# Conditioning products taken two k-tiles at a time in a two-layer hybrid backbone

## The chip, the cores and the metric

The kernel runs on one core of one Trainium2 chip. The metric is device time in microseconds from one launch; a run's time is compared with other runs of the same program on the same chip. Five engines matter here: TensorE (PE for the matmuls, PEld for the weight loads that overlap them), VectorE (DVE), ScalarE (ACT), GpSimd (POOL) and SyncE (SP), which in this kernel issues every DMA.

## The reference

Two layers work on 256 latent tokens and 256 context tokens of width 2048, in float32. Each layer starts with the conditioning: `mod = silu(c) @ ada_w + ada_b`, once for the latent and once for the context vector, which gives a shift, a scale and a gate of 2048 values each. Then

```
h = rms_norm(x, pre_norm) * (1 + scale) + shift
p = h @ w_in            # 5888 columns: attention, RWKV-7, pooling and their gates
y = concat(attention, rwkv, pool) @ w_out
x = x + gate * rms_norm(y, post_norm)
```

`ada_w` has 2048 rows and 6144 columns a layer, so the conditioning multiplies two vectors with 100 MB of weights in all: nearly no arithmetic, and a large share of the kernel's 350 MB of DMA traffic. The shift and scale of layer 0 are wanted at once; the gate of layer 0 and all of layer 1 are not wanted before the end of layer 0.

## The kernel before, in words

All the work is written as generators (workers) that yield operations. A `Scheduler` (`run`) keeps a model of each engine's time, takes at each step the ready operation with the best key, and emits it. What comes out is a fixed order of instructions for each engine; at run time every engine goes through its list in that order and waits on semaphores. So a change in one worker can move any instruction of the program.

The main worker (`main_work`) streams `w_in` and `w_out`: each weight tile is split by ACT and DVE into a high and a low float32r half (tiles `sp`), and PE multiplies three times with the activations (`h`) into `acc`. Around these products the scheduler fits the RWKV scan (`scan`, `pr`), attention (`att`) and the rest.

The conditioning is `ada_work`. For layer 0's shift and scale (`ADA_FIRST`, 8 units of one column part each) weight tiles `w2` of 128 x 512 are used, all before 173 us. For the rest (`ADA_REST`, 8 units of two parts each) a k-tile of 128 rows comes as two tiles `wa` of 128 x 512 (256 KB each). The stationary operand is the conditioning pair, 128 rows by 2 columns, so the array is used in the shape 128*32 (the trace shows 128*2): four column strips j = 0 to 3 hold four outputs that run side by side. The first `wa` of a k-tile feeds strips 0 and 1, the second strips 2 and 3, one product of 256 columns each. So a k-tile is four products, a unit 16 k-tiles, and all units together 128 k-tiles, 256 tiles `wa` and 512 products. When the shape of the array changes between two instructions, the scheduler's model lets the array drain first (`array_free`), and holds the conditioning's products back for a while (`HOLD`), so that they don't cut into the main products too soon.

Tiles `wa` are loaded by `loads`, which takes a token for each k-tile; the main worker hands out 7/8 of a token with each weight tile of two column blocks that it has used (`ADA_RATE`). The pool keeps 4 tiles for `wa` and allows up to 8. Loads go through SP's queue in the order of the scheduler, together with `wf` and `pw` (weights of `w_in`), `tp` (the scan's inputs) and the rest.

Of the kernel before, what the change touches and what calls it, by code (L numbers as in the profile page):

```python
# [21 lines left out]
KT = D // 128  # L22
# [3 lines left out]
T = SEQ + CTX  # L26
# [137 lines left out]
def PASSES(l):  # L164
    return (0, 1) if l < DEPTH - 1 else (1,)
# [29 lines left out]
ADA_FIRST = [(0, quad, [r]) for r in range(4) for quad in range(2)]  # L195
ADA_REST = [(l, q, [2 * h, 2 * h + 1]) for l, q in ((0, 2), (1, 0), (1, 1), (1, 2)) for h in range(2)]
ADA_RATE = 7
LEND = ("at",)
AHEAD = (1, 2)
SLOT = 40.0  # L200
# [8 lines left out]
PRIO = {"setup": 6, "start": 6, "scan": 5, "front": 3, "back": 4, "elim": 4, "fin": 4, "evac": 4, "pre": 4, "gate": 4, "att": 4, "rg": 5, "mix": 5, "load": 1, "ada": 3, "wl": 2, "ws": 6, "main": 0, "norm": 6, "turn": 3, "post": 6}  # L209
# [417 lines left out]
class Hybrid:  # L627
    def __init__(self, ctx, tc, a, log=None):
# [25 lines left out]
        self.nsplit, self.nmain, self.covered = 0, 0, 0  # L654
        self.sch.lend = lambda c: LEND if c == "sp" and self.nsplit < self.covered else ()

# [191 lines left out]
    def ada_work(self):  # L848
        V, S, G, T, D_ = self.V, self.S, self.G, self.T, self.D
        yield self.until("cond")  # L850
        for l, quad, part in ADA_FIRST + ADA_REST:
            n = 128 * len(part)
            ps = yield Alloc("ada", (128, 512))
            for k in range(KT):
                yield Until(lambda: len(self.adaq) > 0)
                for i in range(len(part)):
                    if i:
                        yield Until(lambda: len(self.adaq) > 0)
                    w = self.adaq.pop(0)
                    for j in range(4) if n == 128 else (2 * i, 2 * i + 1):  # L860
                        rhs = w[:, j, :] if n == 128 else w[:, :, j % 2, :]
                        yield T.matmul(out=ps[32 * j:32 * j + 2, 0:n], lhsT=self.cs[:, k, :], rhs=rhs, start=(k == 0), stop=(k == KT - 1))
                    self.free(w)
            sb = self.adasb
            for j in range(4):
                if j % 2:
                    yield V.tensor_copy(out=sb[32 * j:32 * j + 2, 0:n], in_=ps[32 * j:32 * j + 2, 0:n])
                else:
                    yield S.copy(out=sb[32 * j:32 * j + 2, 0:n], in_=ps[32 * j:32 * j + 2, 0:n])
            self.free(ps)  # L870
            yield self.until("vecs", l)
            pt = yield Alloc("ada", (128, 512))
            for b in range(len(part)):
                yield T.transpose(out=pt[:, 128 * b:128 * b + 128], in_=sb[:, 128 * b:128 * b + 128], identity=self.k("ident"))
            for b, r in enumerate(part):
                kt = slice(r, KT, 4)
                src = pt[:, 128 * b:128 * b + 128].rearrange("p (j s) -> p j s", j=4)[:, :, 0:2]
                bias = self.vec(l, "ada_b", 16 * quad, 16)[:, kt].unsqueeze(2).to_broadcast([128, 4, 2])
                yield V.tensor_tensor(out=self.ada[l][:, quad, kt, :], in0=src, in1=bias, op=ALU.add)
                if quad == 1:  # L880
                    pn = self.vec(l, "pre_norm", 0, 16)[:, kt].unsqueeze(2).to_broadcast([128, 4, 2])
                    yield V.scalar_tensor_tensor(out=self.mm[l][:, kt, :], in0=self.ada[l][:, 1, kt, :], scalar=1.0, in1=pn,
                                                 op0=ALU.add, op1=ALU.mult)
            self.free(pt)
            if quad == 2 and part[-1] == 3:
                gp = yield Alloc("tl", (128, KT, 2))
                pn = self.vec(l, "post_norm", 0, 16).unsqueeze(2).to_broadcast([128, KT, 2])
                yield V.tensor_tensor(out=gp, in0=self.ada[l][:, 2], in1=pn, op=ALU.mult)
                ps = yield Alloc("ada", (128, 512))
                yield T.transpose(out=ps[0:32, 0:128], in_=gp.rearrange("p k s -> p (k s)"), identity=self.k("ident"))  # L890
                gs = yield Alloc("tl", (32, 128))
                yield S.copy(out=gs, in_=ps[0:32, 0:128])
                yield D_.dma_start(out=self.gpd[l], in_=gs)
                self.free(gp, ps, gs)
                self.flag("gp", l)
            for r in part:
                self.flag("ada", l, quad, r)
# [222 lines left out]
    def main_in(self, l, gi, left):  # L1120
# [4 lines left out]
        for q in range(4):  # L1125
            for name, i, cb, mode, bs in group:
                for hf in range(2):
# [25 lines left out]
                    if l or gi:  # L1153
                        self.tokens(ADA_RATE * len(bs) / 16)
                    if l == 0 and gi:
# [736 lines left out]
    def run(self):  # L1892
        self.adaq, self.wq, self.sq, self.yq = [], [], [], {}
        self.eq, self.aq, self.fq, self.pq = [], [], [], []
        self.hh, self.hl = {}, {}
        self.startq, self.xtq = [[], []], [[], []]
        self.bq, self.zq, self.rgq, self.q2, self.g2 = [], [], [], [], []
        self.rgat, self.mixat, self.ygs, self.mixs = None, None, {}, {}
        self.lora, self.mx, self.kf, self.vf, self.o = {}, {}, {}, {}, {}
        self.h1 = {s: ({}, {}) for s in range(2)}  # L1900
        sch = self.sch
        sch.add("setup", PRIO["setup"], self.setup())
        sch.add("start", PRIO["start"], self.start_work())
        for s in range(2):
            sch.add("turn%d" % s, PRIO["turn"], self.turn_work(s))
            sch.add("mod%d" % s, PRIO["norm"], self.mod_work(s))
        sch.add("scan", PRIO["scan"], self.scan_work())
        sch.add("front", PRIO["front"], self.front_work(), 16)
        sch.add("back", PRIO["back"], self.back_work(), 16)
        sch.add("elim", PRIO["elim"], self.elim_work())  # L1910
        sch.add("fin", PRIO["fin"], self.fin_work(), 16)
        sch.add("evac", PRIO["evac"], self.evac_work())
        sch.add("pre", PRIO["pre"], self.pre_work())
        sch.add("gate", PRIO["gate"], self.gate_work())
        sch.add("att", PRIO["att"], self.att_work(0))
        sch.add("rg", PRIO["rg"], self.rg_work())
        sch.add("mix", PRIO["mix"], self.mix_work())
        for l in range(DEPTH):
            for s in PASSES(l):
                sch.add("post%d%d" % (l, s), PRIO["post"], self.post_work(l, s), 16)  # L1920
        sch.add("load", PRIO["load"], self.loads())
        sch.add("ada", PRIO["ada"], self.ada_work(), 16)
        sch.add("wl", PRIO["wl"], self.w_loads())
        sch.add("ws", PRIO["ws"], self.w_split())
        sch.add("es", 0, self.early_split())
        sch.add("main", PRIO["main"], self.main_work(), 8)
        with self.tc.manual_schedule():
            sch.run()
# [18 lines left out]
```

## Time and profile before

| | us |
|---|---|
| median of 3 runs | 1771.61 |
| lowest, highest | 1769.43, 1776.53 |
| the profiled execution | 1770.03 |
| its span, first to last instruction | 1768.1 |
| PE busy, in the span | 1675.5 (95%) |
| DVE busy | 1350.8 (76%) |
| ACT busy | 926.8 (52%) |

The span is cut into 40 slices on the profile's page; PE shows nine tenths or more in all but the first and the last two. The mean granted clock of TensorE is 0.981 of the full one. The stage in which the `wa` tiles are used begins with their first product at 172.7 us and ends with the last conditioning instruction at 893.8 us. Behind it come the output product of layer 0, layer 1 and the tail.

### The profile page before, as it was taken

How to read it: one execution, taken by the hardware profiler on the slowest of the kernel's cores; microseconds unless marked ns; L12 is line 12 of the kernel's file. 1: busy time of each engine (PE TensorE's matmuls, PEld its weight loads, DVE VectorE, ACT ScalarE, POOL GpSimd, SP SyncE). 2: the span in 40 equal slices, each digit the busy share in tenths (PEclk: the TensorE clock that was granted, in tenths of full speed). 3: DMA queues.
4: the chain of work that ended last, by engine and by line, in shares of the span. 5: the costliest groups of instructions: out<-in, count | busy, mean ns of one | idle time of the engine just before them, and what ended most of it. 6: DMA issues, size and time to landing. Idle time of an engine off the chain costs nothing.

```text
span 1768.1 us, 38232 instructions
## 1 busy us (share of the span) xinstructions
PE 1675.5 (95%) x13658; PEld 1330.3 (75%) x13658; DVE 1350.8 (76%) x4249; ACT 926.8 (52%) x2278; POOL 16.0 (1%) x93
## 2 busy tenths in 40 slices
PE   4999999999999999999999999999999999999977
PEld 3677677666766676667777888899999888888765
DVE  3335888867897869697767685899689999999863
ACT  5324455434554445345446574575455676666541
POOL 0000000000000000000000000000000000000000
PEclk9999999999999999999999999999999999999988
DMA  9993674657364945574669965665434536555642
GB/s 343 362 365 105 206 227 155 225 185 247 120 221 148 277 149 171 170 238 148 207 223 351 328 191 169 199 202 177 147 102 157 155 98 204 153 165 185 215 132 95
DMA packets 218094, 350.03 MB, mean 198 GB/s; under 512 B 22896, under 2 KB 62128, under 8 KB 217904
## 3 DMA queue, kind: packets, MB, share of 16 engines
q1 hardware_dynamic: 217904, 347.60, 60.2%
q8 instruction: 107, 1.75, 0.4%
q14 instruction: 83, 0.68, 0.1%
HBM read 316.54 MB, written 30.97 MB: 197 GB/s over the span
## 4 chain that ended last, share of the span: by engine, by line
PE 72%; DVE 12%; DMA 10%; ACT 2%; issue 2%; SPq 1%; DVEq 0%; POOL 0%; ACTq 0%
PE acc L587 50%; PE scan L587 6%; PE pr L587 5%; PE att L587 5%; PE ada L587 4%; DVE tp L587 3%; DMA wa<-in_ada_w_dram 2%; DVE sp L587 2%; DMA w<-in_ada_w_dram 2%; DVE q L587 1%; DVE rf L587 1%; DMA wf<-in_w_out_dram 1%; DMA wf<-in_w_in_dram 1%; PE st L587 1%; DMA sp<-w 1%
## 5 line engine op out<-in xcount | busy, mean ns | idle before, releaser
L587 PE MATMUL acc<-h,sp 128*128 128x256 f32 (+1 forms) x5088 | 971.1, 339 | 14.1 <-DMA sp<-w 5.6
L587 PEld LDWEIGHTS acc<-h,sp 128*128 128x128 f32 x5088 | 755.4, 190 | 133.9 <-issue 24.3
L587 DVE TENSOR_TENSOR sp<-wf,sp 128x512 fp32r<-128x512 f32 (+1 forms) x568 | 362.4, 664 | 96.4 <-ACT sp L587 90.2
L587 ACT CAST sp<-wf 128x512 fp32r<-128x512 f32 (+1 forms) x624 | 352.3, 603 | 20.8 <-PE acc L587 7.6
L587 PE MATMUL acc<-sp,h 128*128 128x512 f32 x1152 | 284.6, 403 | 2.9 <-DVE sp L587 2.9
L587 PEld LDWEIGHTS acc<-sp,h 128*128 128x128 f32 x1152 | 216.9, 191 | 54.1 <-DVE sp L587 3.8
L587 DVE TENSOR_TENSOR tp<-tp 128x48 f32<-128x48 f32 (+23 forms) x552 | 133.3, 247 | 5.6
L587 DVE TENSOR_TENSOR tp<-dt,tp 128x48 f32<-128x48 f32 (+23 forms) x496 | 112.0, 226 | 5.6
L587 PE MATMUL ada<-wa,cs 128*2 128x256 f32 x1024 | 85.8, 380 | 6.3 <-DMA wa<-in_ada_w_dram 6.2
L587 ACT CAST pw<-pw 128x512 fp32r<-128x512 f32 x56 | 34.8, 621 | 71.8 <-DMA pw<-in_w_in_dram 59.2
L587 ACT COPY sm<-scan 128x128 f32<-128x128 f32 x64 | 17.0, 265 | 104.4 <-PE scan L587 104.0
L587 DVE TENSOR_TENSOR rf<-tp 64x256 f32<-64x256 f32 x176 | 70.2, 421 | 0.4
L587 DVE STREAM_TRANSPOSE dt<-tp 128x1024 f32<-128x1024 f32 x32 | 65.7, 2077 | 0.0
L587 ACT ACTIVATE aq<-att,q 128x512 f32<-128x512 f32 (+1 forms) x48 | 33.9, 707 | 59.8 <-DVE q L587 49.7
L587 ACT COPY rf<-scan 64x128 f32<-64x128 f32 x128 | 33.2, 259 | 55.6 <-PE scan L587 50.8
L587 DVE SCALAR_TENSOR_TENSOR q<-q 128x4 f32<-128x4 f32 (+3 forms) x378 | 58.3, 159 | 4.2
L587 PEld LDWEIGHTS scan<-rf 128*64 128x64 f32 x896 | 37.3, 137 | 26.2 <-issue 9.2
L587 PE MATMUL ada<-w,cs 128*2 128x128 f32 x1024 | 37.0, 296 | 20.5 <-DMA w<-in_ada_w_dram 19.6
L587 DVE COPY adasb<-ada 2x128 f32<-2x128 f32 (+1 forms) x32 | 11.4, 357 | 57.4 <-ACT adasb L587 50.9
L587 DVE TENSOR_TENSOR pw<-pw 128x512 f32<-128x512 f32 x56 | 38.5, 687 | 21.6 <-ACT pw L587 21.3
L587 PE MATMUL scan<-rf 128*64 128x64 f32 x896 | 49.3, 230 | 4.4 <-DVE rf L587 4.1
L587 ACT COPY tp<-rb 32x128 f32<-32x128 f32 x128 | 37.5, 295 | 28.4 <-DVE rb L587 26.9
(154 smaller groups left out, 1965.7 us busy)
## 6 DMA issues: line engine op xcount, KB each, us to landing
wf<-in_w_in_dram SPq DMA_DIRECT2D x384, 256.0 KB, 3.8
wa<-in_ada_w_dram SPq DMA_DIRECT2D x256, 256.0 KB, 4.2
wf<-in_w_out_dram SPq DMA_DIRECT2D x192, 256.0 KB, 4.5
w<-in_ada_w_dram SPq DMA_DIRECT2D x128, 256.0 KB, 5.3
pw<-in_w_in_dram SPq DMA_DIRECT2D x56, 256.0 KB, 4.8
w<-pw SPq DMA_DIRECT2D x56, 256.0 KB, 2.5
sp<-w SPq DMA_DIRECT2D x56, 256.0 KB, 3.2
wf<-in_w_in_dram SPq DMA_DIRECT2D x48, 128.0 KB, 4.4
```

Of the source, the lines that this page charges most:

```text
L587: op.call(**op.args)
```

## The change

`ada_work` collects the tiles of two k-tiles (`ADA_BATCH = 2`, for the units with `wa` alone) before it yields the first product, then yields the products of the second k-tile and after them those of the first, and frees the four tiles together. The group of accumulations starts and stops with the new first and last product. The number of products, tiles and bytes stays the same, and the worker's window stays 16 operations wide.

```diff
+ADA_BATCH = 2
...
             ps = yield Alloc("ada", (128, 512))
-            for k in range(KT):
-                yield Until(lambda: len(self.adaq) > 0)
-                for i in range(len(part)):
-                    if i:
-                        yield Until(lambda: len(self.adaq) > 0)
-                    w = self.adaq.pop(0)
-                    for j in range(4) if n == 128 else (2 * i, 2 * i + 1):
-                        rhs = w[:, j, :] if n == 128 else w[:, :, j % 2, :]
-                        yield T.matmul(out=ps[32 * j:32 * j + 2, 0:n], lhsT=self.cs[:, k, :], rhs=rhs, start=(k == 0), stop=(k == KT - 1))
-                    self.free(w)
+            size = 1 if n == 128 else ADA_BATCH
+            for k0 in range(0, KT, size):
+                ws = []
+                for _ in range(size * len(part)):
+                    yield Until(lambda: len(self.adaq) > 0)
+                    ws.append(self.adaq.pop(0))
+                for z in range(size):
+                    k = k0 + size - 1 - z
+                    for i in range(len(part)):
+                        w = ws[len(part) * (k - k0) + i]
+                        for j in range(4) if n == 128 else (2 * i, 2 * i + 1):
+                            rhs = w[:, j, :] if n == 128 else w[:, :, j % 2, :]
+                            yield T.matmul(out=ps[32 * j:32 * j + 2, 0:n], lhsT=self.cs[:, k, :], rhs=rhs,
+                                           start=(k0 == 0 and z == 0), stop=(k0 + size == KT and z == size - 1))
+                self.free(*ws)
...
-        sch.add("ada", PRIO["ada"], self.ada_work(), 16)
+        sch.add("ada", PRIO["ada"], self.ada_work(), 8 * ADA_BATCH)
```

The orders are the same up to the first `wa` product. Below, `pr` and `scan` are products of the RWKV part, `acc<-h,sp` main products, `ada<-wa,cs` the conditioning. Three places show what moves.

On PE, shortly after the first `wa` products (at 194 us in the trace), the order of before has:

```order
L587 MATMUL acc<-h,sp 128x512 x3
L587 MATMUL pr<-rf 128x128 x8
L587 MATMUL ada<-wa,cs 2x256 x2
L587 MATMUL acc<-h,sp 128x512 x8
L587 MATMUL pr<-rf 128x128 x8
L587 MATMUL ada<-wa,cs 2x256 x2
L587 MATMUL acc<-h,sp 128x512 x4
```

and the changed one at the same place:

```order
L588 MATMUL acc<-h,sp 128x512
L588 MATMUL pr<-rf 128x128 x8
L588 MATMUL acc<-h,sp 128x512 x10
L588 MATMUL pr<-rf 128x128 x8
L588 MATMUL ada<-wa,cs 2x256 x8
L588 MATMUL acc<-h,sp 128x512 x2
L588 MATMUL pr<-c,rf 128x128 x4
```

Two visits to the conditioning, of two products each, became one visit of eight. Over the whole program, the visits to `ada<-wa,cs` are 112 before (11 of 2 products, 76 of 4, 7 of 6, 18 of 8) and 72 now (8 of 2, 8 of 6, 56 of 8), and the changes of the array's shape from one PE instruction to the next, with the shapes that the trace gives each kind of product, are 808 before and 743 now.

On SP, near the start of the stage, the queue of before has pairs:

```order
L587 DMA pw<-in_w_in_dram 128x512
L587 DMA wa<-in_ada_w_dram 128x512 x2
L587 DMA wf<-in_w_in_dram 128x2x128 x3
L587 DMA rkvd_71<-ev 128x512
L587 DMA wa<-in_ada_w_dram 128x512 x2
L587 DMA pw<-in_w_in_dram 128x512
```

and the changed one, a little further along:

```order
L588 DMA pw<-in_w_in_dram 128x512
L588 DMA w_1_74<-pw 128x512
L588 DMA wf<-in_w_in_dram 128x2x128 x2
L588 DMA wa<-in_ada_w_dram 128x512 x4
L588 DMA w_0_75<-pw 128x512
L588 DMA wf<-in_w_in_dram 128x2x128 x3
```

Rows of four `wa` loads in a stretch number 10 before and 21 now; pairs 99 and 75.

The third place is one where the changed order leaves little between load and use, with the tiles' numbers. SP issues four loads in a row:

```order
L588 DMA wf_6330<-in_w_in_dram 128x512
L588 DMA wa_6403<-in_ada_w_dram 128x512
L588 DMA wa_6409<-in_ada_w_dram 128x512
L588 DMA wa_6406<-in_ada_w_dram 128x512
L588 DMA wa_6412<-in_ada_w_dram 128x512
```

and PE takes the batch apart, the third tile's products ahead and the fourth tile's behind two products of the RWKV part:

```order
L588 MATMUL att_6414<-c_136,aq_6400 128x128 x4
L588 MATMUL ada_5430<-wa_6409,cs_133 2x256 x2
L588 MATMUL pr_6152<-tp_6157,bonesr_137 128x256
L588 MATMUL pr_6152<-tp_6428,bonesr_137 128x256
L588 MATMUL ada_5430<-wa_6412,cs_133 2x256 x2
L588 MATMUL ada_5430<-wa_6403,cs_133 2x256 x2
L588 MATMUL ada_5430<-wa_6406,cs_133 2x256 x2
```

Eight of the 64 batches are split so, into a visit of two products and one of six. Within a k-tile the tile that was pushed first still comes first, so the tile that SP issues last here (6412) is not the one that PE takes first (6409).

## Rows read from the trace of the kernel before

**Rows 1.** The page: the span and each engine's busy time.
```profile
span 1768.1 us, 38232 instructions
PE 1675.5 (95%) x13658; PEld 1330.3 (75%) x13658; DVE 1350.8 (76%) x4249; ACT 926.8 (52%) x2278; POOL 16.0 (1%) x93
```

**Rows 2.** Busy time by stretch: length, each engine (instructions), clock, DMA share, GB/s.
```profile
172.70:893.80 721.10, 708.66 (x5580) 500.41 (x5579) 575.92 (x1897) 352.19 (x894) 7.10 (x44) 0.99 0.60 193
...
1055.40:1702.60 647.20, 615.59 (x5634) 556.12 (x5632) 552.41 (x1823) 387.25 (x980) 7.56 (x38) 0.99 0.52 163
```

**Rows 3.** Chain of waits in the stretch 172.7 to 893.8: shares by line.
```profile
by line: PE acc L587 42.1%; PE att L587 7.9%; PE ada L587 7.9%; PE scan L587 7.7%; PE pr L587 6.7%; DMA wa<-in_ada_w_dram 5.2%; DVE tp L587 4.3%; issue 2.4%; DVE sp L587 2.0%; DVE rf L587 1.6%; DMA pw<-in_w_in_dram 1.5%; DVE q L587 1.4%; DM
```

**Rows 4.** Timeline of PE: start, length, instruction; visits of 4, 8, 12, 16 records.
```profile
195.50 0.60 PE L587 MATMUL ada<-wa,cs 128*2 128x256 f32 x4
196.03 2.14 PE L587 MATMUL acc<-h,sp 128*128 128x512 f32 x8
...
283.70 0.61 PE L587 MATMUL ada<-wa,cs 128*2 128x256 f32 x8
284.25 2.13 PE L587 MATMUL acc<-h,sp 128*128 128x512 f32 x8
...
320.20 1.05 PE L587 MATMUL ada<-wa,cs 128*2 128x256 f32 x16
321.18 0.65 PE L587 MATMUL att<-c,aq 128*128 128x128 f32 x4
...
420.60 1.03 PE L587 MATMUL ada<-wa,cs 128*2 128x256 f32 x12
421.56 0.39 PE L587 MATMUL pr<-tp,bonesr 128*128 128x256 f32 x1
```

**Rows 5.** Timeline of PE: one main product ahead of the same shape, and of another.
```profile
270.95 0.39 PE L587 MATMUL acc<-h,sp 128*128 128x512 f32 x1
271.18 0.86 PE L587 MATMUL att<-at 128*128 128x512 f32 x3
271.87 0.40 PE L587 MATMUL acc<-h,sp 128*128 128x512 f32 x1
272.20 0.69 PE L587 MATMUL scan<-rf 128*64 128x64 f32 x16
```

**Rows 6.** Waits by engine in 172.7 to 893.8: us in total, times, longest.
```profile
PE ada L587 <- DMA wa<-in_ada_w_dram: 6.2, 7, 2.2
PE pr L587 <- ACT tp L587: 2.9, 4, 1.3
...
PEld ada L587 <- DMA wa<-in_ada_w_dram: 14.1, 21, 2.7
```

**Rows 7.** Stretch 172.7 to 893.8, the instructions of tile wa alone.
```profile
172.70:893.80 721.10, 85.72 (x1024) 17.04 (x1024) 0.99 0.60 193
```

**Rows 8.** DMA issues: count, KB each, median us from issue to landing.
```profile
wa<-in_ada_w_dram SPq DMA_DIRECT2D x256, 256.0 KB, 4.2
```

**Rows 9.** Timeline of SP and PE near 680 us; idle time and releaser in brackets.
```profile
680.20 0.94 SPq L587 DMA_DIRECT2D wa<-in_ada_w_dram  x2
...
682.39 0.61 PE L587 MATMUL ada<-wa,cs 128*2 128x256 f32 x8 [1.69 <-DMA wa<-in_ada_w_dram]
...
685.23 1.02 PE L587 MATMUL ada<-wa,cs 128*2 128x256 f32 x4 [2.22 <-DMA wa<-in_ada_w_dram]
...
687.22 1.02 PE L587 MATMUL ada<-wa,cs 128*2 128x256 f32 x4
```

**Rows 10.** Busy time by stretch around the same place; the clock stands behind the engines.
```profile
680.00:684.00 4.00, 1.32 (x12) 0.34 (x10) 3.73 (x15) 0.87 (x2) 0.00 (x0) 0.96 0.91 305
684.00:688.00 4.00, 2.77 (x12) 0.90 (x12) 3.94 (x15) 0.67 (x3) 0.48 (x5) 0.50 0.51 158
688.00:692.00 4.00, 4.00 (x21) 3.59 (x20) 3.52 (x11) 2.85 (x7) 0.14 (x4) 0.68 0.46 148
```

## Prediction

> **What bounds the kernel now.** I read the page first, then the busy time by stretch, then the chain of waits in the one stretch that the change touches, and last the timeline of PE there. PE is busy 95% of the span [rows 1]. In the stretch of the `wa` products, 172.7 to 893.8 us, it is busy 708.7 of 721.1 us, and DVE 575.9 us or 80% [rows 2]. So 12.4 us are left in which PE does nothing, and half of it, 6.2 us, is PE itself standing before a `wa` tile that has not landed [rows 6]; the next in that list, a product that waits for ACT, has 2.9 us. The chain of waits says the same with another weight: five groups of PE work make 42.1 + 7.9 + 7.9 + 7.7 + 6.7 = 72.3% of the stretch, the transfer of `wa` 5.2%, and the rest is DVE work, issue and other transfers in small pieces [rows 3]. In such a stretch time goes away in two ways: PE has less to do, or PE stands less before `wa`. The change touches both, and behind it the orders of all engines are shuffled.
>
> **Part 1: fewer visits.** A visit to the conditioning occupies PE from its first product to the start of the next kind of work. The trace records each of these float32 products twice, so 2, 4, 6 and 8 products are 4, 8, 12 and 16 records. The rows give 196.03 - 195.50 = 0.53 us, 284.25 - 283.70 = 0.55, 421.56 - 420.60 = 0.96 and 321.18 - 320.20 = 0.98 us [rows 4]. Two products cost as much as four, and six as much as eight, because the column strips run side by side: the time goes by steps of one k-tile, begun or whole, not by products. With the counts of the two orders:
>
> before: 11 x 0.53 + 76 x 0.55 + 7 x 0.96 + 18 x 0.98 = 5.8 + 41.8 + 6.7 + 17.6 = 71.9 us;
> now: 8 x 0.53 + 8 x 0.96 + 56 x 0.98 = 4.2 + 7.7 + 54.9 = 66.8 us.
>
> That is 5.1 us less. The eight split batches are the reason that it isn't more: each pays 0.53 + 0.96 instead of 0.98.
>
> **Part 2: fewer changes of shape.** What a change of shape costs the work ahead of it shows in one pair: a main product ahead of another of the same shape takes 271.18 - 270.95 = 0.23 us to the next start, and one ahead of a `scan` product 272.20 - 271.87 = 0.33 us [rows 5], so 0.10 us. The changes fall from 808 to 743, and 65 x 0.10 = 6.5 us. Not all of the 65 are in the stretch: the fall there is larger, and some of it is given back in the output product of layer 0, where scan pieces now stand. The bounds of this term are 0 (if the drain only moves idle time) and 8 us (all 80 changes that 40 visits have at their two ends). I take the 6.5, since the row is an exact pair.
>
> **Part 3: the waits for wa.** The 1024 records of `wa` keep PE busy for 85.7 us [rows 7], and a free run of the same visits would take the 71.9 us of part 1. A visit's last record ends about 0.06 us after the next work starts (0.61 against 0.55), so 112 x 0.06 = 7 us of the 85.7 overlap with the next work. That leaves about 7 us lost inside visits, beside the 6.2 us ahead of them, so some 13 us are in this term; the weight loads' own 14.1 us [rows 6] is the same waiting seen from the other queue and isn't added. A load takes 4.2 us to land [rows 8]. Batching has two effects on it. There are 64 batches to wait for instead of 128 k-tiles, and behind the youngest k-tile the older two tiles are there already. On the other side, a batch waits for the youngest of four tiles instead of two, the four are freed together, and so the next four loads are issued together and closer to their use, as the third place of the order shows. The lower bound is 0, all 13 us gone; the upper bound is twice the present, 26 us, if each batch waits as long as two k-tiles did. I take no change, 13 us, because loads, bytes, tokens and the number of kept tiles are the same, and since the present rows are the nearest to either end.
>
> What stands behind a waiting product is the whole of PE: main products, scan and attention alike, since PE goes through its list in order. DVE is at 80% there and would be the next to be late. SP is passed by more rows of four loads, a megabyte each; the scan's inputs (`tp`) and the weights (`wf`) stand behind those. With the DMA engines at a share of 0.60 in the stretch [rows 2] I cost that at nothing; if the cover is gone, it shows as PE or ACT waiting for `wf` or `tp`.
>
> **Sum.** 5.1 + 6.5 + 0 = 11.6 us of PE work. Of a saving on PE the chain passes on its PE share at least, 72.3% [rows 3]: 8.4 us; all of it would be 11.6. Since PE is busy over 98% of this stretch, I take a value between, 10 us. The profiled execution took 1770.0 us, 1.9 more than its span, and lies 1.6 us under the median of the runs. 1770.0 - 10 = 1760.0, and with the 1.6 us to the median 1761.6. Forecast: 1762 us.
>
> **Stage behind 893.8 us.** Nothing of the change is there, but the order is new. The later stretch has PE idle for 647.2 - 615.6 = 31.6 us [rows 2], more than twice that of the earlier one. A shuffle can move some of that either way; I cost it at nothing and keep 8 us on either side, a quarter of that idle time, as an estimate for the range.
>
> **The rivals.**
>
> First, the saving is handed back as waits. What speaks for it: 28% of the chain in the stretch isn't PE [rows 3], and DVE is at 80%; work that PE no longer hides lets DVE or ACT end last. What speaks against it: PE waited there for others for only 6 us beside `wa`. With half of the 11.6 us kept, 1771.6 - 5.8 = 1766 us, no difference that a measurement of this kernel can tell (about 0.5%, 9 us). Chance 0.35.
>
> Second, the split batches stand and cost the clock. This is the case on the other side. The trace shows its price at one place: two loads issued at 680.20, their products and the next ones start at 682.39 and 685.23 after idle times of 1.69 and 2.22 us [rows 9], and then the granted clock is 0.50, the lower of its two levels (1.2 GHz), in 684 to 688, and 0.68 on average in 688 to 692 [rows 10]; a visit that takes 0.60 then takes 1.02 [rows 4, 9]. Idle time of 1.7 + 2.2 and about 3 us of half speed make 7 us for one place. The order has eight split batches, each with loads issued in a row of four at the most, and a few whole ones with little between load and use. Without the loss of the 13 us changing elsewhere, the gain of 11.6 is gone with two more such places, and the kernel is slower by over 0.5% from three on; with four it is 1771.6 - 11.6 + 28 = 1788 us. Against it: the mean clock of the stretch is 0.99 [rows 2], so half speed lasts at most 0.01 x 721 / 0.5 = 14 us in it, two such places among 112 visits, and those of before may go. Chance 0.14.
> The Trainium skill speaks for this rival: "TensorE: Matmul & The Clock Gate", section "HAM oscillation — how this bites in real kernels", holds that short runs of matmuls between waits for DMA let the clock fall back, and that the fall is paid at each such wait. The trace agrees at 684 us (0.50 behind the two waits) and not in the rest of the stretch, whose mean is 0.99. By that rule, at each of the eight splits, the sum would be 8 x 7 = 56 us worse; by the rows it is one place in 721 us, and I keep the rows.
>
> Third, the waits go too. If one wait for a batch catches the rest, most of the 13 us goes with the 11.6: 1771.6 - 11.6 - 11 = 1749 us. For it: waits are fewer, 64 for 128. Against it: the loads are issued closer to their use. Chance 0.10.
>
> That the change doesn't do what it says is half true already: within a k-tile the older tile still goes first, so in a split batch PE doesn't wait for the youngest tile first. It costs what part 1 has for the splits.
>
> **How the numbers follow.** The forecast has a chance of 0.41, the first rival 0.35, the second 0.14, the third 0.10. Of the forecast's 0.41 a small part, 0.03, lies within 0.5% of before. Faster by over 0.5%: 0.38 + 0.10 = 0.48; within 0.5%: 0.35 + 0.03 = 0.38; slower: 0.14. The range goes from 1750, next to the third rival, to 1774: the first rival's 1766 with the 8 us of the later stage. The second rival is left out above it, and part of the third below.
>
> **What would show it.** In the profile of the changed kernel, right: visits of 16 records at 0.98 us, 56 of them, and PE busy on `wa` at about 80 us or less; PE busy in the whole span down by some 10 us; the stretch from the first `wa` product to the last conditioning instruction shorter by about 10 us; idle time before `wa` near 6 us. Wrong: PE idle before `wa` above 15 us or stretches of the clock at 0.50 beside the one of before (second rival); PE's busy time down and its idle time up by as much on DVE or ACT (first rival); a later stage that moves by more than 8 us, which would mean that the shuffle decides and not the visits.

## The result, and the profile after

| | before | after |
|---|---|---|
| median, us | 1771.98 (4 runs) | 1785.95 (4 runs) |
| lowest, highest | 1769.43, 1776.53 | 1783.34, 1788.66 |
| the profiled execution, and its span | 1770.03, 1768.1 | 1786.87, 1784.8 |

The ratio of after to before is 1.0082, with a 95% interval of 1.0060 to 1.0104. The changed kernel is 14 us slower, where 10 us faster was forecast.

The profile answers in the order of the prediction's steps. First the busy time by stretch (columns as in [rows 2]) of the changed kernel: the old stretch of the `wa` products, the same up to the new last conditioning instruction at 884.5, and the later stretch from the start of layer 1 to its last `scan` product, which holds the same PE work as in [rows 2] (5633 records for 5634). The last row has the instructions of `wa` alone, PE and PEld:

```profile
172.70:893.80 721.10, 704.89 (x5594) 511.91 (x5596) 577.14 (x1900) 355.14 (x897) 7.09 (x44) 1.00 0.61 195
172.70:884.50 711.80, 695.59 (x5524) 505.26 (x5524) 573.80 (x1892) 352.23 (x890) 7.09 (x44) 1.00 0.62 196
1054.30:1720.00 665.70, 625.67 (x5633) 565.79 (x5631) 553.19 (x1823) 388.76 (x980) 7.62 (x38) 0.96 0.50 159
...
172.70:893.80 721.10, 75.08 (x1024) 21.25 (x1024) 1.00 0.61 195
```

The conditioning's stretch is 721.1 - 711.8 = 9.3 us shorter, and PE is busy there for 708.7 - 695.6 = 13.1 us less. The two stretches don't hold quite the same work, though: after's has 64 `scan` records fewer, which PE does later (16 of them in a row take 0.6 to 0.8 us, so some 3 us). The records of `wa` take 75.1 us for 85.7 [rows 7]. A visit of 16 records lasts as long as before (next start less start, 0.97 us in the pair below, from PE's timeline of after):

```profile
323.72 1.04 PE L588 MATMUL ada<-wa,cs 128*2 128x256 f32 x16
324.69 0.96 PE L588 MATMUL acc<-h,sp 128*128 128x512 f32 x3
```

The waits that end PE's idle time in 172.7 to 893.8 (us in total, times, longest), against [rows 6]:

```profile
PE att L588 <- DVE aq L588: 4.6, 5, 2.8
PE ada L588 <- DMA wa<-in_ada_w_dram: 3.5, 4, 1.8
PE pr L588 <- ACT tp L588: 3.4, 4, 1.7
```

So the wait before `wa` did not grow, it fell from 6.2 to 3.5 us. PE's busy time in the whole span did not fall, however: 1675.2 us for the 1675.5 of [rows 1]. Up to here the change did what it says. To see where the gain went I compared the start of the k-th main product (`acc`) in both traces (6240 in each). Offsets are start in the kernel less start in before, in us, worked out from the traces, one execution of each kernel:

```
k of the main product    1950   2210   2340   2730   4680   5070   5200   5590   5720    end
its start in before     818.6  912.9  943.9 1042.9 1361.3 1470.5 1495.3 1580.6 1605.6
after                   -12.1  -10.0   -6.5   -1.1   -0.3  -15.2   +9.8   +1.5  +17.4  +16.8
```

Two losses stand in this line. Of the 10 us by which after is ahead at 913 us, 9 are gone by 980 us, where layer 0 ends. The other 18 us are lost in the second half of layer 1, at two places.

**The end of layer 0.** The chain of waits in 880 to 985 us (start, length, what), of before and then of after:

```profile
927.78 18.12 PE acc L587 x77
945.99 5.96 DMA y<-mixd
...
958.03 5.43 DMA y<-gpd
```

```profile
912.73 5.47 DMA pw<-in_w_in_dram
...
919.72 5.70 DMA pw<-in_w_in_dram
...
928.39 5.36 DMA wf<-in_w_out_dram
933.83 6.07 DMA pw<-in_w_in_dram
...
942.68 5.76 DMA y<-mixd
948.46 0.63 ACT h L588
949.13 8.09 PE acc L588 x28
957.22 5.22 DMA y<-gpd
```

The tiles `y` are filled here from two places: `mixd` is the mixed output of layer 0, the input of the output product, and `gpd` is layer 0's gate, which the conditioning made. Both were written to memory and are read back by the same queue that brings the weights. In after PE was ready earlier, but the chain goes through a row of weight loads, the read of `mixd`, 8 us of main products and the read of `gpd`, and this last one starts at 957.22 for 958.03. The busy time by stretch shows what the transfers had left there, before and then after:

```profile
940.00:980.00 40.00, 37.91 (x157) 30.02 (x156) 28.39 (x47) 25.34 (x50) 0.00 (x0) 0.96 1.03 361
```

```profile
940.00:980.00 40.00, 34.30 (x133) 26.61 (x132) 29.43 (x48) 27.04 (x53) 0.00 (x0) 0.91 1.01 346
```

The DMA engines are full in both (shares of 1.03 and 1.01), and part of what PE had gained stands there as idle time: 40.0 - 34.3 = 5.7 us for 2.1. At main product 2470, behind this place, both kernels have done the same work but for one record, before and then after:

```profile
172.70:978.10 805.40, 790.87 (x5992) 564.81 (x5992) 634.82 (x2010) 400.95 (x992) 7.10 (x44) 0.99 0.63 205
```

```profile
172.70:977.00 804.30, 782.39 (x5991) 571.37 (x5992) 637.24 (x2015) 405.54 (x998) 7.09 (x44) 0.99 0.65 208
```

So for equal work PE is busy 8.5 us less, and idle 21.9 us for 14.5: of the saving, 1.1 us is left. That the transfers hold the end of layer 0 is read from these rows; no run tests it alone.

**Layer 1.** The loss begins behind main product 4680, at 1361 us. PE's busy time from there to the last `scan` product, of before and then of after:

```profile
1361.30:1702.60 341.30, 315.87 (x3154) 276.27 (x3153) 303.13 (x1095) 214.53 (x578) 4.18 (x21) 0.98 0.50 159
```

```profile
1361.00:1720.00 359.00, 325.87 (x3154) 285.77 (x3152) 304.24 (x1095) 216.46 (x578) 4.12 (x21) 0.93 0.48 151
```

The same 3154 records of PE take 17.7 us more: the idle time goes from 25.4 to 33.1 us, and the busy time from 315.9 to 325.9, at a clock of 0.93 for 0.98. PE's timeline at the first place (start, length, idle time and releaser in brackets), of after:

```profile
1467.09 1.68 PE L588 MATMUL att<-aq,at 128*128 128x256 f32 x12
1475.97 1.12 PE L588 MATMUL scan<-c,ts 64*64 64x64 f32 x16 [7.20 <-DVE ts L588]
...
1480.30 2.71 PE L588 MATMUL acc<-h,sp 128*128 128x256 f32 x11
```

and the same two pieces of work in before:

```profile
1459.83 1.58 PE L587 MATMUL att<-aq,at 128*128 128x256 f32 x12
1461.24 5.93 PE L587 MATMUL acc<-h,sp 128*128 128x256 f32 x49
...
1467.56 0.68 PE L587 MATMUL scan<-c,ts 64*64 64x64 f32 x16
```

In before 49 main products stand between the attention and the `scan` product that needs DVE's `ts`; in after none do, and PE stands for 7.2 us. The clock follows (stretches of after, the clock third from the end):

```profile
1471.00:1476.00 5.00, 0.03 (x2) 0.06 (x2) 4.98 (x39) 1.98 (x6) 0.00 (x0) 0.50 0.00 2
1476.00:1488.00 12.00, 12.00 (x72) 11.21 (x73) 8.04 (x29) 5.94 (x16) 0.00 (x0) 0.50 0.11 35
```

At 0.50, the lower of the two levels (1.2 of 2.4 GHz), PE is busy for all of 12 us, and a main product takes 2.71 / 11 = 0.25 us, where the 49 of before took 5.93 / 49 = 0.12. So the 12 us hold about 6 us of work: the place costs 7.2 us of standing and some 6 us of half speed. Nor is it only cover that lacks: the last `ts` that DVE makes for this `scan` product is done at 1475.82 us for 1466.00, so the scan is 10 us late while the main products are 15 us early. The second place reads the same way:

```profile
1598.08 0.45 PE L588 MATMUL scan<-rf,rb 128*64 128x64 f32 x6 [0.47 <-ACT rf L588]
1600.87 0.45 PE L588 MATMUL scan<-rf 128*64 128x64 f32 x2 [2.35 <-DVE rf L588]
1605.14 0.58 PE L588 MATMUL pr<-tp,bonesr 128*128 128x256 f32 x1 [3.82 <-ACT tp L588]
```

Neither place has to do with `wa`: the last of those products was 600 us earlier.

### The profile page after: what moved, and what is told of

Its sections match the earlier page's. It is cut to its first block, busy times and chain, and to the rows that moved or that the text cites. A ratio compares the mean times of both kernels' runs of the same rounds, so it can differ in the third digit from the quotient of the medians.

```text
span 1784.8 us, 38251 instructions
## 1 busy us (share of the span) xinstructions
PE 1675.2 (94%) x13658; PEld 1344.7 (75%) x13658; DVE 1351.3 (76%) x4249; ACT 930.7 (52%) x2278; POOL 16.1 (1%) x93
## 4 chain that ended last, share of the span: by engine, by line
PE 51%; DVE 9%; DMA 6%; ACT 3%; issue 1%; SPq 1%; DVEq 0%; ACTq 0%
PE acc L588 37%; PE scan L588 5%; PE pr L588 4%; PE att L588 3%; DVE tp L588 2%; PE ada L588 2%; DMA wf<-in_w_in_dram 1%; DMA pw<-in_w_in_dram 1%; DVE sp L588 1%; DVE q L588 1%; DVE rf L588 1%; SPq L588 1%; DVE dt L588 1%; DMA y<-mixd 1%; DVE y L588 1%
## 5 line engine op out<-in xcount | busy, mean ns | idle before, releaser
L588 DVE TENSOR_TENSOR tp<-tp 128x48 f32<-128x48 f32 (+24 forms) x552 | 133.2, 247 | 6.0 <-ACT tp L588 0.6
L588 PE MATMUL ada<-wa,cs 128*2 128x256 f32 x1024 | 75.1, 383 | 3.8 <-DMA wa<-in_ada_w_dram 3.5
L588 ACT ACTIVATE aq<-att,q 128x512 f32<-128x512 f32 (+1 forms) x48 | 33.9, 706 | 60.3 <-DVE q L588 43.1
L588 PEld LDWEIGHTS scan<-rf 128*64 128x64 f32 x896 | 38.2, 140 | 25.4 <-issue 9.8
L588 DVE COPY adasb<-ada 2x128 f32<-2x128 f32 (+1 forms) x32 | 11.4, 357 | 59.9 <-ACT adasb L588 55.4
L588 ACT ACTIVATE tp<-tp 128x256 f32<-128x256 f32 x80 | 30.5, 412 | 44.4 <-DVE tp L588 43.7
```

Of the source, the lines that this page charges most:

```text
L588: op.call(**op.args)
```

## The experiments

Theory A: the conditioning is cheaper, as forecast, and the loss is the new order that the scheduler made of layer 1. Rival B: the batch itself costs, since a product waits for the youngest tile of four. To tell them apart, several runs fix the order: the scheduler's choice is replaced by a written list of picks, which can be joined from the lists of two kernels.

```diff
-            best = turn = None
-            for nd in self.ready_nodes.values():
...
+            best = min(self.ready_nodes.values(), key=lambda nd: nd.rank, default=None)
```

**Halves of the two orders.** The first run has the changed order up to main product 2860 (1064 us) and before's order from there; the second has before's order of layer 0, without batching, and the changed order of layer 1.

```diff
+RANKS = picks of after up to ('main', 2860), then picks of before     # first
+RANKS = picks of before up to ('main', 2860), then picks of after     # second
```

> Theory A: the 14 us are lost in layer 1 alone, through the other order that the scheduler made of it (a wait of 7.2 us before one RWKV visit at 1476 us and half clock behind it), and layer 0's gain of 10 us is used up before its end. This kernel has the changed order up to the 2860th main product (1063 us, the end of layer 0) and from there the order of the kernel before. A expects 1771 us (1767 to 1774), no half-clock stretch of 17 us near 1470. Rival B: the batching itself costs, through loads in fours and tiles held longer, whatever layer 1's order: 1786 us (1782 to 1790).

> The reverse: the order of the kernel before, without batching, up to the 2860th main product, then the changed order of layer 1. Theory A (layer 1's order is the loss): 1787 us (1783 to 1791). Rival B (the batching itself is the loss): 1772 us (1768 to 1776).

Measured: 1770.7 us for the first, ratio 1.0008 (0.9992 to 1.0024), and 1783.14 us for the second, ratio 1.0073 (1.0054 to 1.0092). The second has no batch at all and shows the same stop in PE's timeline:

```profile
1464.73 1.69 PE L687 MATMUL att<-aq,at 128*128 128x256 f32 x12
1473.61 1.12 PE L687 MATMUL scan<-c,ts 64*64 64x64 f32 x16 [7.19 <-DVE tp L687]
```

So the loss belongs to layer 1's order, and the batched half without it is no slower than before; it is no faster either. The first run was 11.9 us ahead at main product 2210 and 2.4 ahead at 2470, so the gain was used up at the end of layer 0 as in after. In layer 1 it lost 3.0 us with before's order; the five other runs below whose layer 1 has that order throughout (two of them joined so as well) lost -0.3 to 4.5, which is the spread of one order.

**The batch alone.** Before's order, with each batch of eight products put where its last one stood; everything else as in before.

```diff
+RANKS = picks of before, the 8 products of a batch at the place of the last
```

> The batching alone: the order of the kernel before throughout, only that the eight products of a batch stand together where the last of them stood (66 visits for 112), and that a load follows where its tile comes free later. Theory A with the saving on the path: about 8 us less PE work, 1762 to 1765 us. Theory A with layer 0 ending on the chain of the RWKV scan and not on PE: 1769 to 1772 us, the last scan visit of layer 0 within 3 us of the 927 us of before. Rival B (batching itself costs): 1780 us or more.

Measured: 1804.13 us, ratio 1.0183 (1.0161 to 1.0204). The waits that end PE's idle time in 172.7 to 920 us, and the stretch itself:

```profile
PE att L688 <- DVE aq L688: 12.1, 9, 5.1
PE ada L688 <- DMA wa<-in_ada_w_dram: 11.4, 12, 2.7
...
172.70:920.00 747.30, 706.48 (x5584) 507.33 (x5583) 576.63 (x1897) 351.79 (x896) 7.14 (x44) 0.99 0.58 187
```

This is rival B's range, and its mechanism exists: with the loads nearly where they were (221 of 256 at the same place of SP's queue, the others up to 8 places later), batches wait 11.4 us for their tiles, and 747.3 - 706.5 = 41 us of idle time stand in this stretch, where before has 12.4. It is not what the changed kernel lost by: there the wait was 3.5 us. That the scheduler's other order of loads is the reason is likely, but no run tests it alone. All of this run's loss lies before 920 us; layer 1 keeps before's time.

**One place of layer 1.** The changed order, with the one `scan` visit at 1476 us moved behind the next 25 main products.

```diff
+RANKS = picks of after, the 16 scan<-c,ts at 1476 us after 25 more of 'main'
```

> The changed kernel with one visit moved: the eight products scan<-c,ts before which PE waits 7.2 us at 1469 to 1476 us stand 25 main products later. Theory A: that wait and the half clock behind it cost 7.2 us and about half of 17 us, so 1771 us if all of it goes, 1779 us if the next RWKV product waits in its place for part of it; the half-clock stretch of 17.07 us at 1471 gone or shorter. Rival B (the loss is elsewhere, spread over the program): 1784 to 1788 us.

Measured: 1783.81 us, ratio 1.0063 (1.0041 to 1.0086); by the ratios some 3 us less than the changed kernel, and the intervals overlap. That is above theory A's 1771 to 1779 and at the edge of rival B's 1784 to 1788. The next instruction in the list waits instead:

```profile
1483.48 2.69 PE L689 MATMUL acc<-h,sp 128*128 128x256 f32 x11 [5.67 <-DVE rf L689]
```

One visit doesn't cure the place; what lacks is work ahead of all that hangs on DVE there. In this trace layer 1 lost 10.7 us, for 17.9 in after, but the execution was 9.2 us behind before at main product 2730, where after, with the same order up to 1476 us, was 1.1 ahead. So one order's traces can lie 10 us apart by the end of layer 0, the six runs spread from 1777 to 1790 us, and what the place costs stays open. The loss at the end of layer 0 is in all three traces with after's order there: 9 to 11 us from main product 2210 to 2470 or 2730.

**PE's work taken away.** Before's order, with the `wa` products of the 14 middle k-tiles of each unit left out; then their loads too.

```diff
+                        if n == 128 or k in (0, KT - 1):
+                            yield T.matmul(...)                       # first
...
+                if k in (0, KT - 1):
+                    yield from self.ada_tile(l, quad, part, k)        # second, with the products
```

> The order of before, with 448 of the 512 conditioning products on wa tiles left out (the first and the last k-tile of each unit stay, all loads stay), so PE has about 60 us less to do in layer 0. Question: what sets the end of layer 0, PE's list or the RWKV scan. Theory (the scan's chain of DVE and ACT steps ends last, so a saving on PE ahead of it is used up before the output product): the last scan product of layer 0, at 927 us in before, moves by 25 us at most, PE idle rises by more than half of the 60 us, and the whole takes 1745 to 1768 us. Rival (PE's own work sets the end, as the prediction had it with its 72%): the last scan product moves by 43 to 60 us and the whole takes 1705 to 1730 us.

> As the run without 448 of the 512 conditioning products on wa tiles, in the order of before, but with the 224 loads of those tiles left out as well (59 MB of 348). That run gained nothing. Theory A (layer 0 in a fixed order is a ring in which DVE's, ACT's and the other loads' turns are as tight as PE's): the last scan product of layer 0 stays within 15 us of 927 and the whole is 1755 to 1772 us. Theory B (the loads on SP's queue and the transfers set layer 0's length, so PE's saving alone is worth nothing): the last scan product moves by 30 us or more and the whole is 1720 to 1745 us.

Measured: without the products 1770.2 us, ratio 1.0001 (0.9984 to 1.0019); without the loads as well 1757.65 us, ratio 0.9919 (0.9894 to 0.9945). The stretch of the `wa` products in the first of these, and the waits that end PE's idle time in it:

```profile
172.70:893.80 721.10, 657.57 (x4713) 496.99 (x4712) 576.62 (x1904) 353.23 (x899) 7.14 (x44) 0.97 0.62 194
...
PE att L686 <- DVE aq L686: 22.2, 19, 8.3
PE pr L686 <- ACT tp L686: 13.4, 8, 3.2
PE acc L686 <- DVE sp L686: 7.0, 7, 2.1
```

PE is busy 708.7 - 657.6 = 51 us less, at a clock of 0.97 for 0.99, and the program is no shorter: the interval leaves 3 us either way. The theory of the first expectation held on its place, the scan, and by its bound on the idle time; the time itself lies 2 us above its range. The last `scan` product of layer 0, in before, then without the products, then without products and loads:

```profile
927.10 0.68 PE L587 MATMUL scan<-c,ts 64*64 64x64 f32 x16
```

```profile
924.65 0.68 PE L686 MATMUL scan<-c,ts 64*64 64x64 f32 x16
```

```profile
909.53 0.68 PE L685 MATMUL scan<-c,ts 64*64 64x64 f32 x16
```

With the loads gone too it moves by 17.6 us, so the transfers hold part of it, but most of the 75 us or so of `wa` work (7/8 of 85.7) has cover from other work in a fixed order: by the waits above, DVE's and ACT's turns are nearly as late as PE's. The 17.6 lie just above the 15 of the ring theory and well below the 30 of the other.

**Other orders from the same scheduler.** One constant of the planner, the time for which it holds the conditioning's products back, was set to 2500 and to 3500 in both kernels; a fifth run is the changed kernel with the older k-tile first.

```diff
-HOLD = {None: 1000.0, "ada": 3000.0}
+HOLD = {None: 1000.0, "ada": 2500.0}      # and 3500.0; in before and in after
...
-                    k = k0 + size - 1 - z
+                    k = k0 + z              # the fifth, hold 3000
```

> The kernel before, without batching, with the planner's hold on the conditioning's products at 2500 instead of 3000. A small rule of the planner that has nothing to do with layer 1, whose order is drawn anew all the same. Theory (layer 1's time is that of whatever order falls out; the batching has no part in it): the second half, from main product 2860 on, differs from before's by more than 5 us in one direction or the other, and the whole lies anywhere from 1758 to 1790 us. Rival (layer 1 is robust and it is the batching that made its order worse): the second half is within 3 us of before's and the whole within 1766 to 1778 us.

> The changed kernel with the hold at 2500 instead of 3000. Theory (layer 1's order falls out by chance): layer 1 differs from the changed kernel's by more than 5 us, with other places of PE idle before DVE or ACT, and the whole lies anywhere from 1762 to 1795 us; the gain up to main product 2210 stays at 5 us or more. Rival (batching makes layer 1 worse): layer 1 loses 12 to 18 us against before again, the whole 1782 to 1790 us.

> The changed kernel with the older k-tile of a batch first, so that only the turn within the batch is undone. If taking the last landed tile first is what keeps batches whole and the waits low, the visits split: more than 20 visits of fewer than 16 records instead of 16, PE idle before wa above 6 us and the conditioning's last instruction 5 us or more later than the 884.5 of the changed kernel. If the turn has no part in it, the visits are as in the changed kernel and the idle time before wa is 2 to 5 us. For layer 1 the theory (order by chance) expects a second half that differs from the changed kernel's by more than 5 us, the rival (batching makes it worse) 1782 to 1790 us in all.

> The kernel before, without batching, with the planner's hold at 3500 instead of 3000. Theory (each new order of layer 1 is a draw with a spread of tens of us, whatever moved it): layer 1 loses anything from 5 to 50 us against before's, the whole 1770 to 1820 us, while the wait before the wa tiles stays at 4 to 10 us. Rival (the loss at 2500 came from the shorter hold itself, which lets the conditioning cut in sooner): a longer hold leaves layer 1 within 5 us of before's, the whole 1762 to 1778 us.

> The changed kernel with the hold at 3500 instead of 3000. Theory (draw): layer 1 again loses another amount than with 3000 (17.9 us) and 2500 (10.4 us), anything from 5 to 50 us, while the stretch of the wa products keeps its gain of 5 us or more at main product 2210. Rival (the size of the loss follows from the batch and the hold in one direction, longer hold, more loss): 20 to 30 us in layer 1, the whole 1785 to 1800 us.

Measured, with the offset of the main products as above (us ahead is negative), and how many of the 8164 picks from main product 2860 on are before's, counted up to the first that differs:

```
                          median   ratio (95% interval)      k=2210  k=2730    end   layer 1   same picks
after, hold 3000         1785.95   1.0082 (1.0060, 1.0104)    -10.0    -1.1  +16.8     +17.9          327
batching, hold 2500      1770.80   1.0004 (0.9990, 1.0018)    -29.7    -8.4   +1.9     +10.3          327
batching, hold 3500      1799.90   1.0181 (1.0151, 1.0212)    -26.4   -12.4  +30.7     +43.1          187
batching, older first    1814.10   1.0242 (1.0216, 1.0267)     -0.5    -4.0  +42.0     +46.0         2684
no batching, hold 2500   1811.09   1.0229 (1.0205, 1.0252)     -0.1    -3.0  +38.5     +41.5          169
no batching, hold 3500   1764.15   0.9959 (0.9940, 0.9978)    -14.2    -5.6   -4.6      +1.0         5634
```

Layer 1's loss needs no batching: the kernel without it loses 41.5 us there by a constant that concerns layer 0 alone, and at 1811 us lies even above its theory's 1758 to 1790. The five orders that leave before's within 2684 picks lost 10 to 46 us in layer 1, and the one that follows it for 5634 lost 1.0. That last run refutes my expectation for it (I had looked for a loss, since I took every order to be a new one) and meets its rival's numbers (within 5 us, 1762 to 1778 us); it agrees with the theory only once the order is counted, which I did afterwards. The rival's reason, that a shorter hold brings the loss, fails with batching, where 2500 lost least. For the hold of 3500 with batching the rival's size fails (43.1 for 20 to 30), but its direction holds among the batched orders: 10.3, 17.9 and 43.1 us rise with the hold. Without batching there is no such direction: 41.5, 0 and 1.0. Three points don't rule it out. The older k-tile first gave 66 visits of fewer than 16 records for the changed kernel's 16, 4.2 us before `wa` (the sign was more than 6), and the last conditioning instruction at 891.9 us for 884.5. So taking the last first does keep the batches whole, though not by the wait; but at main product 2730, behind layer 0, this kernel was no worse (-4.0 for -1.1).

What the bad orders share is in PE's timeline. From main product 2860 to the last one PE is idle for 31.6 us in before and the half clock lasts 24 us; in the five orders that lose, the idle time is 34 to 51 us and the half clock 44 to 113 us; in the sixth, 30.5 and 31. The run with the older k-tile first, at 1519 us:

```profile
1517.79 0.68 PE L588 MATMUL pr<-tp,rb 32*32 32x32 f32 x32 [6.67 <-DVE tp L588]
...
1519.86 1.12 PE L588 MATMUL scan<-rf 128*64 128x64 f32 x16
1521.65 0.69 PE L588 MATMUL scan<-sm,rb 64*64 64x64 f32 x8 [0.67 <-ACT sm L588]
1522.69 1.71 PE L588 MATMUL scan<-rf,rb 128*64 128x64 f32 x16 [0.35 <-ACT rf L588]
1525.19 1.54 PE L588 MATMUL scan<-rf 128*64 128x64 f32 x16 [0.79 <-DVE rf L588]
1526.94 0.69 PE L588 MATMUL scan<-sm,rb 64*64 64x64 f32 x8 [0.20 <-ACT sm L588]
...
1519.00:1537.00 18.00, 13.18 (x167) 10.84 (x168) 4.06 (x15) 4.50 (x18) 0.00 (x0) 0.50 0.01 2
```

Behind a stop of 6.67 us the steps of the scan stand bare, one behind the other, each with a wait for ACT or DVE between, at a clock of 0.50. The main products that covered them in before were spent ahead of time: this run is 21.8 us ahead at main product 5070 and 53.4 behind at 5200, as after is 15.2 ahead and then 9.8 behind.

**Layer 0 with batching, layer 1 of before.** The heads of the two batched orders with other holds, joined to before's order from main product 2860 on.

```diff
+RANKS = picks of batching, hold 2500, up to ('main', 2860), then of before   # first
+RANKS = picks of batching, hold 3500, up to ('main', 2860), then of before   # second
```

> The order of the changed kernel with the hold at 2500 up to main product 2860 (layer 0 and its output product, with batching), and from there the order of before. The kernel with the hold at 2500 was 8.5 us ahead of before at that product and lost it in layer 1. Theory (the layers add, each with its own order): the 8.5 us stay to the end but for up to 3 us that the seam costs, as it did in the first hybrid: 1762 to 1766 us, faster than before. Rival (layer 1's order of before fits only the state that before's layer 0 leaves, or the end of layer 0 is bounded elsewhere): 1769 us or more.

> The order of the changed kernel with the hold at 3500 up to main product 2860, and from there the order of before. The kernel with the hold at 3500 was 12 to 15 us ahead of before from main product 2730 on until 4680, and then lost 43 us in layer 1. Theory (a gain of layer 0 can reach the end in full when its own last pieces don't stand in the way and layer 1 keeps a good order): 9 to 15 us ahead to the end, 1756 to 1762 us. Rival (however layer 0 is ordered, some 5 us at most pass its end, as in the two hybrids before): 1765 us or more.

Measured: 1763.34 us, ratio 0.9962 (0.9949 to 0.9976), and 1761.7 us, ratio 0.9938 (0.9918 to 0.9959). Both beat both kernels; the second is 10 us faster than before. Its page, and its group of `wa` products (busy us, mean ns of one, idle time before them):

```profile
span 1760.4 us, 38241 instructions
...
PE 1661.0 (94%) x13658; PEld 1338.6 (76%) x13658; DVE 1350.4 (77%) x4249; ACT 926.7 (53%) x2278; POOL 15.9 (1%) x93
...
L689 PE MATMUL ada<-wa,cs 128*2 128x256 f32 x1024 | 71.5, 378 | 2.1 <-DMA wa<-in_ada_w_dram 1.9
```

PE is busy 14.5 us less than in [rows 1] and `wa` takes 71.5 us. It is 8.6 us ahead at main product 2730 and 8.0 at the end, a little under the 9 to 15 expected. The end of layer 0 is therefore no wall at 5 us, as the rival had it; the order there decides. How much of the 10 us is due to batching is not shown: before's kernel with the hold at 3500, without any, gained 7 us, and the two intervals overlap.

## Why the prediction was wrong

**Part 1, fewer visits (-5.1 us): right.** Visits of 4, 12 and 16 records are 8, 8 and 56 in the trace, at 0.53, 0.96 and 0.97 us in the median. The 71.9 us for before were too low, as single rows stood for whole groups: from first product to the next kind of work its visits take 82.6 us, and after's 71.2 for the 66.8 reckoned. The difference is time lost inside the visits, which part 3 has.

**Part 2, fewer changes of shape (-6.5 us): the price holds, the sum is not shown.** A main product ahead of a `wa` visit takes 0.33 us in the median of 52 pairs in before, and 0.23 ahead of another main product. But PE's 13.1 us less in the stretch are no proof of the 11.6 of parts 1 and 2: scan work is missing there, and waiting inside visits is in it. For equal work, at main product 2470, PE is busy 8.5 us less.

**Part 3, the waits for wa (no change): too cautious, and inside its bounds.** The 13 us became some 7.5: PE's idle time before `wa` fell from 6.2 to 3.5 us (4.1 of the 6.2 stood between products of a visit, not ahead of visits as I had read it), and of slow running inside the visits, reckoned as before, 75.1 - 72 x 0.06 - 66.8 = 4.0 us are left of 7. The loads landed in 4.0 us for 4.2 [rows 8]. That was luck: the batch alone waited 11.4 us, and before's kernel with the hold at 3500, which has no batches, waits 3.5 too.

**The sum ("the chain passes on its PE share at least, 72.3%"): failed.** 9.3 us came out of the stretch, nine tenths of the forecast and some of it only work put off, but 1.1 us were left behind the end of layer 0. A share of the chain that ended last [rows 3] is no rate at which a saving passes on. The run without the products shows how far off: 51 us off PE, nothing off the program. Chains through DVE, ACT and the transfers end almost as late, by the waits of that run, and a chain of waits shows only the last of them. The first rival, "the saving is handed back as waits", described this; I gave it half of the gain, and it took nine tenths.

**"Stage behind 893.8 us: cost at nothing, +-8 us": failed, and this decided the sign.** Layer 1 lost 17.9 us. I had sized the term by a quarter of the idle time there, 31.6 us [rows 2]. But a bad order doesn't move idle time about, it makes new idle time and half the clock with it: of the 17.7 us by which the stretch from 1361 us grew, 7.7 are idle time and 10.0 the same work at a lower clock. The six orders above put the term at +1 to +46 us, and five of the six above 8. With that spread, slower would have been the likelier side. The prediction had named the sign, a later stage that moves by more than 8 us, but gave it no chance of its own.

**The second rival (split batches cost the clock): right on the sign, wrong on the place.** Its price for one place, 7 us, was about half of the 13 us read at the first place of layer 1; but the split batches stood in a stretch with a clock of 1.00, and the slow clock came in layer 1, behind waits for DVE and ACT. Slower was right here by luck.
The Trainium skill, in "TensorE: Matmul & The Clock Gate", section "HAM oscillation — how this bites in real kernels", ties the slow clock to matmuls that come in short runs between waits. The rows of 1471 to 1488 us agree in part: 0.50 behind one wait of 7.2 us, which was for DVE in the place of its waits for DMA, and with no short runs ahead of it.

**What I should have read.** The third place of the orders in the part on the change showed that other engines' rows move too, but I compared the orders only around the conditioning. A look at layer 1's PE rows would have shown the missing main products ahead of `scan<-c,ts`. I didn't test whether that look alone would have given the sign.

What stays open: which change in layer 0 sends the scheduler into a bad order of layer 1. It is shown that the order does it, not how the choice comes about. And the two losing places of after were not priced one by one, since moving one visit moved the wait along.

## What to carry to other kernels

Where a scheduler lays out the whole program, a local change is two changes: its own effect, and a new order of everything behind it; measure them apart by fixing the order, and take the spread of the second from orders that a neutral constant gives. A PE at 95% says that it is well covered, not that taking work from it shortens anything: ask which other chain ends within the saving. And once a good order for a stage is known, keep it: half of one joined to half of another was worth 10 us here.

## What the runs showed of the hardware

The slow clock can outlive the wait that brings it: behind a stop of 7.2 us PE ran 12 us at 0.50 although it was busy all the time, so the stop cost nearly twice its length. Behind another stop, of 6.67 us, scan steps with gaps of 0.2 to 0.9 us between them ran at 0.50 for all of the 18 us shown.

The same reads took longer where the DMA engines were full. Four reads of `gpd`, 256 KB each, landed in 5.6 us (before) and 5.4 us (after) in the median at 955 to 965 us, at a DMA share of 1.09 and 1.05; the next four took 4.3 and 4.2 us at 1040 to 1050 us, at 0.87 and 0.83. No run varied the load alone.
